# First stage in sweeps over half tiles, with 128-byte table pieces, and the last half stored in two pieces

## The chip, the cores and the metric

The kernel runs on one core of a Trainium2 chip. The metric is the device time of one execution in microseconds. The engines are TensorE (PE in the profile, with PEld for its weight loads), VectorE (DVE), ScalarE (ACT), GpSimd (POOL) and SyncE (SP); SP and ACT also issue DMA transfers, each on a queue of its own that is worked off in order.

## What is computed

One layer of a decoder: `h = x + RMSNorm_post(mixer(RMSNorm_pre(x)))` with 512 tokens of 1024 numbers, all in fp32. The mixer is a sparse attention with 16 heads in 4 groups and three branches: over compressed keys and values, over selected blocks, and over a window. With 512 tokens every block is selected. The parts that matter here:

```
u = rms_norm(x, pre_gain)
q, kv, g, z = split(u @ w_in)
kc = compress_kv(k_c, k_pos, k_w1, k_w2)     # blocks of 32 tokens, stride 16:
vc = compress_kv(v_c, v_pos, v_w1, v_w2)     # silu((block + pos) @ w1) @ w2
bias = table[t5_bucket(dist)]                # one table 32 x 16, for all three branches
o = three softmax branches; y = sum(sigmoid(g) * o * silu(z)); out = x + rms_norm(y @ w_out, post_gain)
```

## The kernel before

Every product is made of three matmuls, since fp32 operands are split in a high part (rounded to fp32r) and a low part (what is left): high by high, low by high, high by low. The normed input is kept as `uh` and `ul`, transposed, features on partitions. Weights come in tiles of 128 x 4 x 256 (512 KB) through `load_raw` into three buffers `wr`; `split_raw` casts the high part `wh` and subtracts to the low part `wl`, each with three buffers. A list `order` names the first twenty tiles: two for compressed keys (w0, w1), two for compressed values (w2, w3), then in turn four tiles for the attention values and four of the key MLP, and so on. In `split_ahead` even tiles have their high part cast on ScalarE and their low part on GpSimd, odd ones both on VectorE.

The first stage does this. `rms(t)` squares a tile of 128 tokens on ScalarE (L306) and takes the reciprocal root on GpSimd (L86, L90). `prep(t)` scales it on VectorE by that and by the gain, which lies in two PSUM banks (L316), transposes it on TensorE (L321), and splits it on ScalarE (L327) and VectorE (L328). The projection of compressed keys runs in two halves of 256 tokens, over all eight feature tiles (L247 to L249), so the first half needs input tiles 0 and 1 and both weight tiles, and tiles 2 and 3 are prepared inside it. `tables()` is called behind the first half: it multiplies the bias table with one-hot rows into `toep` (L344, L345) and, in sixteen matmuls of 16 columns (L351, L352), into `cb`; both are stored to DRAM (`toepd`, L347; `cmpb`, L356, in pieces of 16 bytes) and read back in the form of `bias` and `cbs` tiles by `load_bias(0)` (L163, L168). After the second half of keys come the position rows (`load_pos`), the key blocks (`blocks`, L407: eight VectorE operations that read the two banks of keys, then splits on ScalarE, VectorE and GpSimd), the projection of compressed values with 512 columns at a time (`half_t`), and the value blocks. Then follows the projection of attention values (L480 to L482, four banks) in turn with the key MLP (L425 to L427). The rest, attention woven with further projections, and the output projection, follows an order that a planner in the code writes out.

The end: `wout` closes the four token tiles in the order 0, 3, 2, 1. For the last one, two VectorE operations (L874, 512 columns each) add the residual, and each is followed by a store of 256 KB on SP's queue.

Engines work their queues in order. The framework orders instructions by its own estimate of time, except those pinned by `keep_in_program_order`.

Of the kernel before, what the change touches and what calls it, by code (L numbers as in the profile page):

```python
# [19 lines left out]
S = 512  # L20
# [3 lines left out]
G = 4  # L24
# [27 lines left out]
def nsa_layer(ctx: ExitStack, tc: tile.TileContext, x, pre_gain, post_gain, table, w_in, w_out,  # L52
# [39 lines left out]
    uh = [keep.tile([128, 2, S], F32R, name=f"uh{i}", tag="u", bufs=8) for i in range(4)]  # L92
    ul = [keep.tile([128, 2, S], F32R, name=f"ul{i}", tag="u", bufs=8) for i in range(4)]
# [46 lines left out]
    def proj_t(w, m, p):  # L140
        hi, lo = w
        ms = slice(m * 128, m * 128 + 128)
        for k in range(KT):
            a, b = hi[k // 4][:, k % 4, ms], lo[k // 4][:, k % 4, ms]
            rh, rl = uh[k // 2][:, k % 2, :], ul[k // 2][:, k % 2, :]
# [105 lines left out]
    def half_t(n, kh, banks):  # L251
        h, l = tile_(n)
        for kk in range(4):
            k = kh * 4 + kk
            for m, p in enumerate(banks):
                ms = slice(m * 128, m * 128 + 128)
                pass3(p, h[:, kk, ms], l[:, kk, ms], uh[k // 2][:, k % 2, :], ul[k // 2][:, k % 2, :],
                      k == 0, k == KT - 1)

    with tc.tile_pool(name="a1", bufs=1) as a1:  # L260
# [38 lines left out]
        banks = [tb, ob, tb]  # L299
        nb_ = 0  # L300

        rs_ = {}

        def rms(t):
            ss = a1.tile([128, 1], F32, name="ss", bufs=4)
            tc.keep_in_program_order(A.activation(sq, xs[t], AF.Square, scale=1.0 / 32, accum_out=ss))  # L306
            r = a1.tile([128, 1], F32, name="r", bufs=4)
            rstd(r, ss)
            rs_[t] = r

        def prep(t):
            nonlocal nb_
            r = rs_[t]
            for kq in range(2):
                hs = slice(kq * 512, (kq + 1) * 512)
                V.scalar_tensor_tensor(xs[t][:, hs], xs[t][:, hs], r, gain[kq], op0=ALU.mult, op1=ALU.mult)  # L316
                p = banks[nb_ % 3]()
                nb_ += 1
                for j in range(4):
                    k = kq * 4 + j  # L320
                    T.transpose(p[:, j * 128:(j + 1) * 128], xs[t][:, k * 128:(k + 1) * 128], ident)  # L321
                for jj in range(2):
                    i = kq * 2 + jj
                    src = p[:, jj * 256:(jj + 1) * 256].rearrange("p (a b) -> p a b", a=2)
# [702 lines left out]
```

## Time and profile before

| | us |
|---|---|
| median of three runs (lowest, highest) | 466.47 (466.29, 467.47) |
| the profiled execution | 466.85 |
| its span (first to last instruction of the profile) | 465.0 |
| TensorE busy in the span | 450.9 |
| VectorE, ScalarE, GpSimd busy | 330.6, 274.3, 184.7 |

All times in the profile count from the start of the span. A row of a timeline gives start, duration and, in brackets, how long the engine had been idle and what it waited for. Matmuls overlap, so the pace is read from start to start and not from the duration. The granted clock (PEclk) is 1.00 at TensorE's upper level, 2.4 GHz, and 0.50 at the lower one, 1.2 GHz.

### The profile page before, as it was taken

How to read it: one execution, taken by the hardware profiler on the slowest of the kernel's cores; microseconds unless marked ns; L12 is line 12 of the kernel's file. 1: busy time of each engine (PE TensorE's matmuls, PEld its weight loads, DVE VectorE, ACT ScalarE, POOL GpSimd, SP SyncE). 2: the span in 40 equal slices, each digit the busy share in tenths (PEclk: the TensorE clock that was granted, in tenths of full speed). 3: DMA queues.
4: the chain of work that ended last, by engine and by line, in shares of the span. 5: the costliest groups of instructions: out<-in, count | busy, mean ns of one | idle time of the engine just before them, and what ended most of it. 6: DMA issues, size and time to landing. Idle time of an engine off the chain costs nothing.

```text
span 465.0 us, 6924 instructions
## 1 busy us (share of the span) xinstructions
PE 450.9 (97%) x2330; PEld 375.3 (81%) x2330; DVE 330.6 (71%) x801; ACT 274.3 (59%) x642; POOL 184.7 (40%) x185
## 2 busy tenths in 40 slices
PE   5999999999999999999999999999999999999994
PEld 4797888878888878888888788888878888888883
DVE  6869844851766888768769776885896667567685
ACT  5712232542766577767846867666776666467541
POOL 4424544242223453342463525245343342448212
PEclk9989999999999999999999999999999999999998
DMA  8489275263111321511132332024051211214113
GB/s 300 142 82 280 77 216 162 66 206 90 47 45 48 112 59 34 182 45 47 45 90 70 88 94 71 21 57 132 19 180 45 92 45 47 91 43 140 47 45 135
DMA packets 45501, 44.63 MB, mean 96 GB/s; under 512 B 7751, under 2 KB 38471, under 8 KB 45466
## 3 DMA queue, kind: packets, MB, share of 16 engines
q1 hardware_dynamic: 44424, 44.00, 31.9%
q8 instruction: 18, 0.29, 0.3%
q10 hardware_dynamic: 1042, 0.20, 0.2%
q14 instruction: 17, 0.14, 0.1%
HBM read 41.99 MB, written 2.20 MB: 95 GB/s over the span
## 4 chain that ended last, share of the span: by engine, by line
PE 89%; DVE 4%; ACT 3%; issue 2%; POOL 1%; DVEq 0%; POOLq 0%; ACTq 0%
PE ps_pj L146 11%; PE ps_pj L148 11%; PE ps_pj L147 11%; PE ps_s L591 9%; PE ps_t L681 7%; PE ps_o L715 4%; PE ps_o L714 4%; PE ps_pj L834 3%; PE ps_pj L835 3%; PE ps_pj L836 3%; PE ps_s L247 2%; PE ps_s L248 2%; PE ps_s L249 2%; PE ps_pj L247 2%; PE ps_pj L248 1%
## 5 line engine op out<-in xcount | busy, mean ns | idle before, releaser
L118 POOL TENSOR_TENSOR wl<-wr,wh 128x512 fp32r<-128x512 f32 x94 | 123.0, 1328 | 138.6 <-ACT wh L113 122.2
L146 PE MATMUL ps_pj<-uh,wh 128*128 128x512 f32 x240 | 99.0, 412 | 0.0
L148 PE MATMUL ps_pj<-ul,wh 128*128 128x512 f32 x240 | 94.2, 393 | 0.0
L147 PE MATMUL ps_pj<-uh,wl 128*128 128x512 f32 x240 | 94.2, 392 | 0.0
L604 ACT ACTIVATE p<-p,nm 128x512 f32<-128x512 f32 (+3 forms) x128 | 71.6, 560 | 24.3 <-DVE nm L603 23.5
L685 DVE TENSOR_TENSOR ptl<-ps_t,pth 128x512 fp32r<-128x512 f32 x80 | 55.0, 688 | 28.2 <-ACT pth L684 27.7
L113 ACT CAST wh<-wr 128x1024 fp32r<-128x1024 f32 x47 | 49.2, 1047 | 43.5 <-DMA wr<-in_nsa_w_in_dram 20.1
L591 PE MATMUL ps_s<-kd,q 128*128 128x512 f32 (+5 forms) x256 | 63.9, 336 | 0.7 <-DVE zs L699 0.6
L684 ACT CAST pth<-ps_t 128x512 fp32r<-128x512 f32 x80 | 46.4, 580 | 29.3 <-PE ps_t L681 28.7
L148 PEld LDWEIGHTS ps_pj<-ul,wh 128*128 128x128 f32 x240 | 45.1, 188 | 10.1
L591 PEld LDWEIGHTS ps_s<-kd,q 128*128 128x128 f32 x256 | 43.9, 189 | 9.0 <-DVE zs L699 1.2
L146 PEld LDWEIGHTS ps_pj<-uh,wh 128*128 128x128 f32 x240 | 45.2, 188 | 6.1
L147 PEld LDWEIGHTS ps_pj<-uh,wl 128*128 128x128 f32 x240 | 45.3, 189 | 5.8
L603 DVE CUSTOM_DVE_ANT_0 p<-ps_s,bias 128x128 f32<-128x128 f32 (+3 forms) x80 | 34.6, 447 | 20.7 <-PE ps_s L591 20.5
L681 PE MATMUL ps_t<-ident,p 128*128 128x128 f32 x320 | 48.4, 272 | 0.0
L681 PEld LDWEIGHTS ps_t<-ident,p 128*128 128x128 f32 x320 | 39.7, 140 | 9.4
L714 PE MATMUL ps_o<-pth,vt 128*128 128x512 f32 x80 | 33.7, 421 | 0.0
L603 DVE CUSTOM_DVE_ANT_1 p<-ps_s,bias 128x256 f32<-128x256 f32 (+2 forms) x48 | 26.3, 555 | 9.3 <-PE ps_s L591 8.6
L728 POOL TENSOR_TENSOR y<-otmp,zs 128x256 f32<-128x256 f32 x16 | 12.3, 771 | 51.5 <-DVE otmp L725 51.5
L715 PE MATMUL ps_o<-ptl,vt 128*128 128x512 f32 x80 | 32.3, 404 | 0.0
L730 POOL TENSOR_TENSOR otmp<-otmp,zs 128x256 f32<-128x256 f32 x15 | 11.1, 741 | 37.9 <-DVE otmp L725 37.9
L569 ACT ACTIVATE zs<-ps_pj 128x512 f32<-128x512 f32 x22 | 13.1, 596 | 19.4 <-PE ps_pj L148 19.3
(268 smaller groups left out, 895.6 us busy)
## 6 DMA issues: line engine op xcount, KB each, us to landing
wr<-in_nsa_w_in_dram SPq DMA_DIRECT2D x36, 512.0 KB
wr<-in_nsa_w_in_dram SPq DMA_DIRECT2D x16, 256.0 KB
bias<-toepd SPq DMA_DIRECT2D x16, 256.0 KB
wr<-in_nsa_w_out_dram SPq DMA_DIRECT2D x8, 512.0 KB
xt<-in_x_dram SPq DMA_DIRECT2D x4, 512.0 KB
wr<-in_nsa_cmp_k_w_dram SPq DMA_DIRECT2D x4, 512.0 KB
wr<-in_nsa_cmp_v_w_dram SPq DMA_DIRECT2D x4, 512.0 KB
xr<-in_x_dram SPq DMA_DIRECT2D x8, 256.0 KB
```

What stands on the lines that cost most here:

```text
L113: A.copy(h[:, 0:kn], raw[:, 0:kn])
L118: el.tensor_tensor(l[:, ks], raw[:, ks], h[:, ks].bitcast(F32), op=ALU.subtract)
L146: T.matmul(p, a, rh, start=k == 0, stop=False)
L147: T.matmul(p, b, rh, start=False, stop=False)
L148: T.matmul(p, a, rl, start=False, stop=k == KT - 1)
L591: T.matmul(po, qs[h][:, qt * 128:(qt + 1) * 128], kds[h // R][:, i, c0:c0 + n], start=i == 0, stop=i == 1)
L603: V.tensor_tensor_reduce(pd, src, bi, 1.0, BIG, ALU.add, ALU.min, st["nm"][:, hh:hh + 1])
L604: A.activation(po, po, AF.Exp, bias=st["nm"][:, hh:hh + 1], scale=-1.0, accum_out=st["rs"][:, hh:hh + 1])
L681: T.transpose(tp[:, hh * 128:(hh + 1) * 128], st["p"][hh][:, c:c + 128], ident)
L685: V.tensor_tensor(pl, tp, ph.bitcast(F32), op=ALU.subtract)
L714: T.matmul(acc, v, ph, start=j == 0, stop=False)
L715: T.matmul(acc, v, pl, start=False, stop=j == qt)
```

## The change

The input tiles 0 and 1 come in halves of 512 features, w1 comes behind tile 2, and w2 behind tile 3. Of tile 0's square the second half is made on VectorE. `uh` and `ul` are two tiles of four feature tiles each instead of four of two, and one cast and one subtraction split 512 columns at a time. The projection runs in sweeps, each of one weight tile, one half of the features and 256 tokens: 24 matmuls, first high by high, then `ul` by high, then `uh` by `wl`. The sweeps go keys 0, keys 1, values 0 on the first 256 tokens, then the same on the last 256. Everything in the stage is pinned in program order. The value banks are now of the kind `o`; since half of each is written first, a matmul of a zero row opens each (`open_`). `tables()` comes behind the sixth sweep, its matmuls before and inside the second half of the value projection; the stores come behind that, `cmpb` in pieces of 128 bytes, and `load_bias(0)` is called behind the attention values. Odd tiles from the fifth on have their high part cast on ScalarE, tile 3 is split on ScalarE and GpSimd. At the end the last half is made in two operations of 256 columns, the first stored by ScalarE's queue, the second by SP's.

```
-            tiles.append(split_raw(raws[i], 4, *((V, V) if i % 2 else (A, P))))
+            tiles.append(split_raw(raws[i], 4, *((A, V) if i % 2 and i > 3 else (A, P))))
...
+        zrow = a1.tile([1, 128], F32R, name="zrow")
+        V.memset(zrow.bitcast(F32), 0.0)
         for t in range(NT):
             xt = a1.tile([128, D], F32, name="xt", bufs=4)
-            SP.dma_start(xt, x[t * 128:(t + 1) * 128, :])
+            for c in ((slice(0, 512), slice(512, D)) if t < 2 else (slice(0, D),)):
+                SP.dma_start(xt[:, c], x[t * 128:(t + 1) * 128, c])
             xs.append(xt)
-            if t == 1:
-                load_ahead(1)
+            if t:
+                load_ahead(t - 1)
...
+            for c, acc in ((0, ss), (512, s2)):
+                xc, junk = xs[t][:, c:c + 512], sq[:, c:c + 512]
+                if t == 0 and c:
+                    put(V.tensor_tensor_reduce(junk, xc, xc, 1.0 / D, 0.0, ALU.mult, ALU.add, acc))
+                else:
+                    put(A.activation(junk, xc, AF.Square, scale=1.0 / 32, accum_out=acc))
+            rstd(rs_[t], ss, s2)
...
+        def open_(ps_):
+            for p in ps_:
+                put(T.matmul(p, zrow, gh[:, 0:S], start=True, stop=False))
+
+        def sweep(n, ps_, kq, hs, opened=False):
+            h, l = tiles[n]
+            for w, u in ((h, uh), (h, ul), (l, uh)):
+                for kk in range(4):
+                    for m, p in enumerate(ps_):
+                        put(T.matmul(p[:, hs], w[:, kk, m * 128:(m + 1) * 128], u[kq][:, kk, hs],
+                                     start=not opened and kq == 0 and w is h and u is uh and kk == 0,
+                                     stop=kq == 1 and w is l and kk == 3))
+                yield
...
+        norm(1, 1, ob)
+        low(1, 0)
+        p_kc = [pj(), pj()]
+        run(sweep(0, p_kc, 0, h0))
...
+        run(sweep(0, p_kc, 0, h1))
+        with tc.issue_after(behind[0]):
+            kpt = load_pos("k")
+            vpt = load_pos("v")
+        run(sweep(1, p_kc, 1, h1))
+        kb = blocks(p_kc, kpt)
+        run(sweep(2, p_vc, 0, h1, True))
+        with tc.issue_after(behind[0]):
+            tables()
...
-        p_vc = [sb(), sb()]
-        half_t(2, 0, p_vc)
         half_t(3, 1, p_vc)
-        vb = blocks(p_vc, vpt)
-        kw2h, kw2l = load_w2("k", 2)
-        vw2h, vw2l = load_w2("v", 1)
+        SP.dma_start(toepd, toep)
+        for g in range(G):
+            SP.dma_start(dview(cmpb, g * H * MC * R, [[8 * R, 128], [1, 8 * R]]),
+                         small["cb"][:, g].rearrange("p j r -> p (j r)"))
+        vb = block_split(blocks(p_vc, vpt))
...
+        load_bias(0)
         hs = silu2(p_mk)
...
-        for i in range(2):
-            finish(*prev, i)
+        t, xr, ss = prev
+        finish(t, xr, ss, 0)
+        for c, q_ in ((0, A), (256, SP)):
+            cs = slice(c, c + 256)
+            last(V.scalar_tensor_tensor(xr[1][:, cs], g3[1][:, cs], ss, xr[1][:, cs], op0=ALU.mult, op1=ALU.add))
+            q_.dma_start(out[t * 128:(t + 1) * 128, S + c:S + c + 256], xr[1][:, cs])
```

What this does to the order of instructions is shown at three places. The first is TensorE at the start, from its first transposes on; `xt` is an input tile, `ps_t` and `ps_o` are banks for transposes, `ps_pj` the banks of compressed keys. Before:

```order
L321 MATMUL ps_t<-ident,xt 128x128 x4
L321 MATMUL ps_o<-ident,xt 128x128 x4
L321 MATMUL ps_t<-ident,xt 128x128 x4
L247 MATMUL ps_pj<-uh_80,wh 128x256
L248 MATMUL ps_pj<-uh_80,wl 128x256
```

and now:

```order
L349 MATMUL ps_t<-ident,xt 128x128 x8
L349 MATMUL ps_o<-ident,xt 128x128 x8
L386 MATMUL ps_pj<-uh_80,wh 128x256 x8
L386 MATMUL ps_pj<-ul_82,wh 128x256 x8
L386 MATMUL ps_pj<-uh_80,wl 128x256 x8
L386 MATMUL ps_pj<-uh_81,wh 128x256 x8
L386 MATMUL ps_pj<-ul_83,wh 128x256 x8
L349 MATMUL ps_t<-ident,xt 128x128 x4
L386 MATMUL ps_pj<-uh_81,wl 128x256 x8
L349 MATMUL ps_t<-ident,xt 128x128 x4
L379 MATMUL ps_o<-gh,zrow 128x512 x2
L386 MATMUL ps_o<-uh_80,wh 128x256 x8
```

The matmuls stand in runs of eight of one kind, the fourth group of transposes has moved ahead of the first matmul, and those of tile 2 stand between runs.

The second place is VectorE between the key blocks (`blk<-ps_pj`) and the value blocks (`blk<-ps_s`, now `ps_o`); `toep` and `cb` are the tables, `bl` the low parts of blocks. Before:

```order
L407 TENSOR_TENSOR blk<-ps_pj,ptk 64x16x31 x8
L115 CAST wh<-wr 128x1024
L118 TENSOR_TENSOR wl<-wr,wh 128x512
L417 TENSOR_TENSOR bl<-blk,bh 128x496 x2
L118 TENSOR_TENSOR wl<-wr,wh 128x512
L407 TENSOR_TENSOR blk<-ps_s,ptv 64x16x31 x8
```

and now:

```order
L274 TENSOR_TENSOR blk<-ps_pj,ptk 64x16x31 x8
L407 COPY toep<-ps_s 16x512
L407 COPY toep<-ps_s 16x128
L118 TENSOR_TENSOR wl<-wr,wh 128x512 x2
L414 COPY cb<-ps_s 128x8x4x4
L499 TENSOR_TENSOR bl<-blk,bh 128x496 x2
L274 TENSOR_TENSOR blk<-ps_o,ptv 64x16x31 x8
```

The three table copies, which stood ahead of the key blocks, have moved behind them, and the cast has gone.

The third place is SP's queue around the table transfers; `wr` are weight tiles, of which those of 128x2x256 come in pairs and are the tiles of attention values. Before:

```order
L103 DMA wr<-in_nsa_w_in_dram 128x2x256 x2
L103 DMA wr<-in_nsa_cmp_k_w_dram 128x4x256
L347 DMA toepd<-toep 16x640
L356 DMA cmpb<-cb 128x8x4 x4
L163 DMA bias<-toepd 128x512 x4
L168 DMA cbs<-cmpb 128x1x128 x4
L103 DMA wr<-in_nsa_w_in_dram 128x2x256 x2
```

and now:

```order
L537 DMA toepd<-toep 16x640
L103 DMA wr<-in_nsa_w_in_dram 128x2x256
L539 DMA cmpb<-cb 128x32 x4
L103 DMA wr<-in_nsa_w_in_dram 128x2x256
L163 DMA bias<-toepd 128x512 x2
L103 DMA wr<-in_nsa_cmp_k_w_dram 128x4x256
L163 DMA bias<-toepd 128x512 x2
L168 DMA cbs<-cmpb 128x1x128 x4
L163 DMA bias<-toepd 128x512 x2
L103 DMA wr<-in_nsa_w_in_dram 128x2x256 x2
L103 DMA wr<-in_nsa_cmp_k_w_dram 128x4x256
```

Before, the stores and the first loads of tables stood behind the first pair; now they stand around the third pair and the third MLP tile, ahead of the fourth pair.

## Rows read from the trace of the kernel before

**Rows 1.** Page, part 1: busy us (share of the span) xinstructions.
```profile
PE 450.9 (97%) x2330; PEld 375.3 (81%) x2330; DVE 330.6 (71%) x801; ACT 274.3 (59%) x642; POOL 184.7 (40%) x185
```

**Rows 2.** Stretches: us, PE, PEld, DVE, ACT, POOL busy; PEclk, DMA share, GB/s.
```profile
0.00:10.00 10.00, 5.15 (x16) 3.55 (x16) 6.05 (x16) 5.66 (x10) 4.07 (x14) 1.00 0.85 306
```

**Rows 3.** Timeline of PE: start, us, engine, line, names, shapes, count [idle before <-releaser].
```profile
6.96 1.12 PE L321 MATMUL ps_t<-ident,xt 128*128 128x128 f32 x4 [1.92 <-DVE xt L316]
...
7.86 1.06 PE L321 MATMUL ps_o<-ident,xt 128*128 128x128 f32 x4
...
10.24 0.58 PE L247 MATMUL ps_pj<-uh,wh 128*128 128x256 f32 x1 [0.46 <-ACT uh L327]
...
16.51 0.66 PE L321 MATMUL ps_o<-ident,xt 128*128 128x128 f32 x4 [0.41 <-DVE xt L316]
...
16.92 0.36 PE L248 MATMUL ps_pj<-uh,wl 128*128 128x256 f32 x1
...
19.16 0.63 PE L321 MATMUL ps_t<-ident,xt 128*128 128x128 f32 x4 [0.57 <-issue]
...
22.77 0.27 PE L351 MATMUL ps_s<-nth,hcr 33*128 33x16 f32 x1
...
24.64 0.58 PE L247 MATMUL ps_pj<-uh,wh 128*128 128x256 f32 x1
...
28.01 0.32 PE L247 MATMUL ps_pj<-uh,wh 128*128 128x256 f32 x1
...
41.94 0.39 PE L480 MATMUL ps_pj<-wh,uh 128*128 128x512 f32 x1
...
44.98 0.47 PE L480 MATMUL ps_s<-wh,uh 128*128 128x512 f32 x1 [0.61 <-DVE blk L407]
...
63.41 0.40 PE L480 MATMUL ps_pj<-wh,uh 128*128 128x512 f32 x1
```

**Rows 4.** Timeline of PE, more rows for the pace of matmuls.
```profile
28.17 0.28 PE L248 MATMUL ps_pj<-uh,wl 128*128 128x256 f32 x1
...
30.44 0.28 PE L249 MATMUL ps_pj<-ul,wh 128*128 128x256 f32 x1
...
32.39 0.39 PE L247 MATMUL ps_s<-uh,wh 128*128 128x512 f32 x1
```

**Rows 5.** Stretch behind the narrow table matmuls.
```profile
25.00:26.00 1.00, 1.00 (x6) 1.00 (x6) 0.72 (x4) 0.00 (x0) 0.35 (x1) 0.50 0.26 71
```

**Rows 6.** Timelines of ACT, DVE, DVE and POOL at the start.
```profile
4.00 1.06 ACT L306 ACTIVATE sq<-xt 128x1024 f32<-128x1024 f32 x1 [1.23 <-DMA xt<-in_x_dram]
...
2.92 1.27 DVE L293 TENSOR_TENSOR gl<-grow,gh 1x512 fp32r<-1x512 f32 x2
...
6.15 2.18 DVE L316 SCALAR_TENSOR_TENSOR xt<-xt,r,ps_s 128x512 f32<-128x512 f32 x3 [1.96 <-POOL r L90]
...
5.24 0.22 POOL L86 TENSOR_SCALAR r<-ss 128x1 f32<-128x1 f32 x1 [3.92 <-ACT sq L306]
```

**Rows 7.** Groups by form, 0:45: xcount | busy us, mean ns | idle
```profile
L407 DVE TENSOR_TENSOR blk<-ps_pj,ptk 64x496 f32<-64x496 f32 x8 | 5.4, 672 | 0.1
```

**Rows 8.** Timeline of PE, last wait for a weight tile.
```profile
91.89 0.38 PE L427 MATMUL ps_o<-wl,bh 128*124 128x256 f32 x1 [0.36 <-DVE wl L118]
```

**Rows 9.** Timeline of SP: issue of table loads and of the fourth value tile.
```profile
28.34 2.50 SPq L163 DMA_DIRECT2D bias<-toepd  x4
...
30.88 5.54 SPq L168 DMA_DIRECT2D cbs<-cmpb  x4
...
55.70 0.88 SPq L103 DMA_DIRECT2D wr<-in_nsa_w_in_dram  x2
```

**Rows 10.** Stretches at the end of the span.
```profile
462.25:462.50 0.25, 0.00 (x0) 0.00 (x0) 0.00 (x0) 0.00 (x0) 0.00 (x0) 0.50 0.64 246
...
463.00:463.25 0.25, 0.00 (x0) 0.00 (x0) 0.00 (x0) 0.00 (x0) 0.00 (x0) 0.50 1.04 385
...
463.75:464.00 0.25, 0.00 (x0) 0.00 (x0) 0.00 (x0) 0.00 (x0) 0.00 (x0) 0.50 0.04 8
```

More of the change, by code (lines that the diff above doesn't have):

```diff
@@ L298, in nsa_layer @@
         sq = a1.tile([128, D], F32, name="sq")
-        banks = [tb, ob, tb]
-        nb_ = 0
-        rs_ = {}
+        put = tc.keep_in_program_order
+        rs_, pt_, behind = {}, {}, []
         def rms(t):
             ss = a1.tile([128, 1], F32, name="ss", bufs=4)
[L306 to L324, printed above, removed]
-                    dh = uh[i][:, :, t * 128:(t + 1) * 128]
-                    dl = ul[i][:, :, t * 128:(t + 1) * 128]
-                    A.copy(dh, src)
-                    V.tensor_tensor(dl, src, dh.bitcast(F32), op=ALU.subtract)
@@ new lines, in rms, with scale, turn_, norm @@
+            rstd(rs_[t], ss, s2)
+        def scale(t, kq):
+            xt = xs[t][:, kq * 512:(kq + 1) * 512]
+            put(V.scalar_tensor_tensor(xt, xt, rs_[t], gain[kq], op0=ALU.mult, op1=ALU.mult))
+        def turn_(t, kq, home):
+            xt = xs[t][:, kq * 512:(kq + 1) * 512]
+            p = pt_[t, kq] = home()
+            for j in range(4):
+                put(T.transpose(p[:, j * 128:(j + 1) * 128], xt[:, j * 128:(j + 1) * 128], ident))
+        def norm(t, kq, home):
+            scale(t, kq)
+            turn_(t, kq, home)
@@ new lines, in part, with high, low, split_first @@
+        def part(u, t, kq):
+            return u[kq][:, :, t * 128:(t + 1) * 128], pt_[t, kq].rearrange("p (a b) -> p a b", a=4)
+        def high(t, kq):
+            put(A.copy(*part(uh, t, kq)))
+        def low(t, kq):
+            d, p = part(ul, t, kq)
+            i = put(V.tensor_tensor(d, p, part(uh, t, kq)[0].bitcast(F32), op=ALU.subtract))
+            behind[:] = [i.ins]
+        def split_first(n, el=P):
+            h = wp.tile([128, 4, 256], F32R, name="wh", tag="wh", bufs=3)
+            l = wp.tile([128, 4, 256], F32R, name="wl", tag="wl", bufs=3)
+            put(A.copy(h, raws[n]))
+            tiles.append((h, l))
+            def rest(i):
+                ks = slice(i * 2, i * 2 + 2)
+                put(el.tensor_tensor(l[:, ks], raws[n][:, ks], h[:, ks].bitcast(F32), op=ALU.subtract))
+            return rest
@@ L365, in nsa_layer @@
+        high(0, 0)
+        norm(0, 1, tb)
+        w0 = split_first(0)
+        w0(0)
+        w0(1)
+        norm(1, 0, ob)
+        low(0, 0)
+        high(1, 0)
+        norm(1, 1, ob)
+        low(1, 0)
+        p_kc = [pj(), pj()]
+        run(sweep(0, p_kc, 0, h0))
+        high(0, 1)
+        high(1, 1)
+        low(0, 1)
+        low(1, 1)
         rms(2)
+        w1 = split_first(1, V)
+        w1(0)
+        w1(1)
         rms(3)
[L367 to L379 removed]
+        w2 = split_first(2)
@@ new lines, in nsa_layer @@
+        w2(0)
+        w2(1)
+        s1 = sweep(1, p_kc, 1, h0)
+        next(s1)
+        next(s1)
+        norm(2, 0, tb)
+        high(2, 0)
+        run(s1)
+        norm(2, 1, tb)
+        high(2, 1)
+        scale(3, 0)
+        low(2, 0)
+        low(2, 1)
+        p_vc = [ob(), ob()]
+        open_(p_vc)
+        s2 = sweep(2, p_vc, 0, h0, True)
+        next(s2)
+        turn_(3, 0, tb)
+        high(3, 0)
+        scale(3, 1)
+        next(s2)
+        turn_(3, 1, tb)
+        high(3, 1)
@@ L798, in split_y @@
             else:
-                yhl[g] = [keep.tile([128, 2, S], F32R, name=f"y3{i}", tag="u", bufs=8) for i in range(2)]
+                t = keep.tile([128, 2, 2, S], F32R, name="y3", tag="u", bufs=4)
+                yhl[g] = [t[:, i] for i in range(2)]
         sl = slice(qt * 128, (qt + 1) * 128)
@@ L821, in wout @@
         turn = [0, 3, 2, 1]
-        og = [keep.tile([128, D], F32, name="og", tag="u", bufs=8) for _ in range(NT)]
+        og = [t[:, i] for t in [keep.tile([128, 2, D], F32, name="og", tag="u", bufs=4) for _ in range(2)] for i in range(2)]
         sumsq = const.tile([128, NT, 2], F32, name="sumsq")
```

102 lines of the change are left out of this document (49 added, 53 removed).

## The prediction

> **What bounds the kernel now.** I read the page's busy times first: TensorE is busy for 450.9 of 465.0 us [rows 1], so all idle time together is 14 us, and a change to order and transfers can win back only a part of that. Then the stretches: 4.85 us of it lie in the first 10 us [rows 2]. Then TensorE's timeline: the first projection matmul starts at 10.24 and the first matmul of the value projection (L480) at 41.94 [rows 3]; I call these 31.70 us the first stage. Inside it the reader is to see three kinds of loss. Idle ones: 0.41 us before 16.51 and 0.57 before 19.16, where transposes of tiles 2 and 3 wait [rows 3]. Slow ones: 16 table matmuls of 16 columns run from 22.77 to 24.64, and behind them 15 matmuls of 256 columns take the 3.37 us to 28.01 [rows 3], 0.22 us each, while the granted clock is 0.50, the 1.2 GHz level [rows 5]; from 28.17 to 30.44 nineteen steps of the same kind take 0.1195 us each [rows 4]. So the lower clock cost 3.37 - 15 x 0.1195 = 1.58 us. And small ones where transposes, tables and matmuls alternate. After the stage there are two idle places left that matter: 0.61 us before 44.98, for a PSUM bank that VectorE's block copies hold, and 0.36 before 91.89, for a low half of a weight tile [rows 3, 8].
>
> From the value projection on, the order of TensorE's instructions is the same in both kernels but for the places of a few matmuls in its first group. So I forecast the first stage, carry its gain through as a shift, and look for what could break the shift.
>
> **The start.** Halving the input lets the squares start on half a tile, but the last half still lands at 4.00 us, when ScalarE starts now [rows 6], because the same bytes come in the same order. VectorE takes the second half of tile 0 and is busy with the gain's low half until 4.19 [rows 6]; one 512-column pass is 0.73 us (2.18 for three [rows 6]), so it ends at 4.95, where before the squares released GpSimd at 5.24 [rows 6]. The rstd on GpSimd took 0.91 us from 5.24 to VectorE's start at 6.15 [rows 6]. The first transposes then start at about 6.7 instead of 6.96 [rows 3], 0.25 us earlier. That gain is lost again: the sweep begins only behind all sixteen transposes of tiles 0 and 1, where before the first matmul followed twelve. VectorE's new order is three scales, a low half, the fourth scale: 5.9 + 3 x 0.73 = 8.1, a wait for ScalarE's 512-column cast until 8.5, then 0.69 for the low half (a 512-element pass of this kind is bounded by 0.67 [rows 7] and 0.73) and 0.73 for the scale give 9.9; four transposes take 0.9 us (6.96 to 7.86 [rows 3]). The first sweep starts at about 10.8, 0.6 us later than now.
>
> **The first stage itself.** From there TensorE has to do: 144 matmuls of 256 columns (96 for keys, 48 for the first half of values) x 0.1195 = 17.2; 24 of 512 columns for the second half of values x 0.2274 (32.39 to 41.94 in 42 steps [rows 3, 4]) = 5.5; four groups of four transposes at 0.41 (16.51 to 16.92 [rows 3]) = 1.6; the two zero matmuls that open the value banks, 2 x 0.2274 = 0.45; the sixteen narrow ones 1.87 (22.77 to 24.64); the four wide table matmuls and two small transposes by the same pace 0.9; two matmuls at the lower clock before it rises, 0.2. Sum 27.7. Of this the zero matmuls are new, and so is the cutting of the first half of values: 48 x 0.1195 against 24 x 0.2274 is 0.28 us more. The Trainium skill's TensorE: Matmul & The Clock Gate (section "Wait — 56ns, not 53.3ns?") puts the fixed cost of one more warm matmul at about 2.5 ns; by it the cutting would cost an estimated 0.06 us and the sum would be 0.2 lower. The rows here give 11 ns per cut, and I stay with them.
>
> Waits: the scale of tile 2 stands behind the low half of the second weight tile on VectorE, which I work out to hold TensorE for 0.15 us. At the end a new one appears. The narrow table matmuls need a bank that VectorE's copy of the first table empties, and that copy now stands behind the eight block copies of the keys (0.672 each, 5.4 us [rows 7]). These start when the fifth sweep ends, at about 28.1, so the table copy ends at 34.25; TensorE comes there, after the sixth sweep (2.9), the wide tables (0.7) and ten matmuls (2.3), at 33.9, and waits 0.4. With 0.4 us for changes between kinds of matmul (what the old stage lost beside the waits named, about) the stage takes 27.7 + 0.15 + 0.4 + 0.4 = 28.65 us and ends at 10.8 + 28.65 = 39.45 against 41.94: **2.5 us** saved. Of these, 1.58 is the low clock, 0.98 the two idle places, the rest of the old alternation pays for the later start and the new matmuls.
>
> **What hides the rest.** The casts of odd weight tiles move from VectorE to ScalarE; VectorE loses about 0.7 us each, ScalarE has room (274 us busy of 465 [rows 1]). The cover for VectorE's work is the second half of values: it must finish key blocks, table copies, one low half and two low block parts before the value blocks can start; I get about 39.3 against TensorE's 39.45, so the 0.61 us bank wait stays as it is, and each 0.1 us that VectorE is later adds 0.1. The bound is 0.7 on one side (one more pass of that kind [rows 7]) and nothing on the other, since the bank wait can't start before TensorE is there. The 0.36 us before 91.89 should go: VectorE's chain of kd parts and that low half has one cast of 0.7 us less in it. Bounds 0 to 0.36; I take 0.36.
>
> **The end.** The last half is written in two pieces on two queues. The last two stores move 512 KB without a gap from 462.25 to 463.75 at 246 to 385 GB/s, and 1.2 us pass between the last bytes and the span's end [rows 10]. The bytes, their start (the first store is unchanged) and the last VectorE result stay, so the end of the transfer stays: 0. If smaller last pieces did shorten the path, the bound is half a store's time, 128 KB at about 370 GB/s = 0.35 us gain; if the second queue costs something, about as much loss.
>
> **Sum.** 2.5 + 0.36 + 0 = 2.85 us off the profiled execution's 466.85 (span 465.0 and 1.85 around it) is 464.0. The median of the three runs is 466.47, 0.38 lower, inside their spread of 1.2 us, so I don't shift for it fully and say **464.1**.
>
> **Rivals.** *The clock falls again* behind the narrow table matmuls. For it: they stand together again, with the 0.4 us wait ahead of them, so the quiet stretch is 2.3 us instead of 1.87. Against: at their old place tables, transposes and matmuls also alternated, and now full matmuls stand right before and behind. Price 1.58 less the little that VectorE's lag gives back: 464.1 + 1.5 = 465.6. *The low clock lasts through the first sweep* because TensorE's first 10 us stay thin: 24 matmuls at 0.22 instead of 0.1195 cost at most 2.3, with half of that 465.3, with all 466.4. *The sweeps don't close the gaps*: ScalarE or VectorE is the bound between 11 and 21 us (a sweep's weight cast stands behind a square of 1.06 us [rows 6] on ScalarE) and each of the six sweeps waits 0.4: 464.1 + 2.4 = 466.5, no change. *Weights wait behind tables* (the slower side). SyncE's queue is in order, and the fourth value tile's load now stands behind six bias and four cbs loads, with the four cmpb stores a little ahead. Before, four and four of these kept the queue for 2.50 + 5.54 us [rows 9], and the fourth value tile's load, issued at 55.70, was used at 63.41, 7.7 us later [rows 9, 3]. In the new kernel that use would be at 39.45 + 21.5 = 60.9, so the load must go by 53.2. The table loads follow the third MLP tile, at about 43.7; at the old pace (8.0 + 0.9 for two more bias loads) they are through at 52.6, 0.6 in time. The mechanism decides from there, 1 us for 1 us; at 1.6 times the old pace it costs 4.8: 468.9. Against it: the 16-byte pieces of cmpb that filled the DMA engines before are now 128 bytes and an eighth as many, and the wait for their completion was part of the 5.54. The Trainium skill's DMA: Bandwidth & Descriptors (section "Specifications") holds against this that transfers under 512 B are below line rate, which 128 B still is; by that rule the stores would stay dear, and the loads behind them late, which is this rival; no row here shows 128-byte pieces.
>
> **How the numbers follow.** Forecast (clock stays up) 0.47; clock falls again 0.30; long low clock at the start 0.08; gaps stay 0.07; weights behind tables 0.08. About 0.3%, 1.4 us, is what a measurement of this kernel can tell from no change: 465.07 and 467.87 are the edges. Faster: nearly all of the first, a quarter of the second, half of the third, 0.57. Slower: the last, with a little for the unforeseen, 0.09. Between: 0.34. The range runs from the forecast less the tail's 0.35 and an error of 0.6 in a stage of 28.65 us, 463.2, up through the second and most of the third case, 466.2; it leaves out the rest of the third, the fourth and the last.
>
> **What would show it.** First sweep's start near 10.8 and unbroken 256-column matmuls at 0.12 us; first value-projection matmul near 39.5 (41 if the clock fell, with 0.50 in the stretches after the narrow matmuls); a wait of 0.4 us on VectorE before the first narrow one; the bank wait still about 0.6; no wait before the last key-value MLP tile; the same distance of 1.2 us from the last byte to the end. Wrong it would be if the order that is the same behind the first stage met new waits on weights, or if the first sweeps waited for casts.

## The result, and the profile after

The changed kernel takes 470.09 us (median of six runs, 469.85 to 472.86), the kernel before 467.37 in the same session: a ratio of 1.0079, with a 95% interval from 1.0055 to 1.0102. It is some 3 us slower (2.7 by the medians, 3.7 by the ratio), where I had forecast 2.4 us faster, and outside my range. The profiled execution took 470.27 us (span 468.5), 3.4 more than that of the kernel before, and TensorE is busy for 3.5 us more than in [rows 1]:

```profile
PE 454.4 (97%) x2356; PEld 378.9 (81%) x2356; DVE 321.4 (69%) x784; ACT 283.7 (61%) x647; POOL 186.2 (40%) x187
```

So the time is not lost in waits alone: TensorE itself works longer. Where, its timeline shows. The rows answer to those of the first stage in [rows 3]; the columns are start, duration, engine, line, names, shapes and count.

```profile
7.19 1.97 PE L349 MATMUL ps_t<-ident,xt 128*128 128x128 f32 x8 [2.15 <-DVE xt L343]
9.92 2.37 PE L349 MATMUL ps_o<-ident,xt 128*128 128x128 f32 x8 [0.76 <-DVE xt L343]
11.94 1.78 PE L386 MATMUL ps_pj<-uh,wh 128*128 128x256 f32 x8
13.56 1.11 PE L386 MATMUL ps_pj<-ul,wh 128*128 128x256 f32 x8
...
36.29 0.40 PE L412 MATMUL ps_s<-nth,hcr 33*128 33x16 f32 x1
...
40.19 0.49 PE L248 MATMUL ps_o<-uh,wl 128*128 128x512 f32 x1
...
40.91 0.63 PE L247 MATMUL ps_o<-uh,wh 128*128 128x512 f32 x1
41.33 0.63 PE L248 MATMUL ps_o<-uh,wl 128*128 128x512 f32 x1
...
45.08 0.39 PE L563 MATMUL ps_pj<-wh,uh 128*128 128x512 f32 x1
```

The first sweep starts at 11.94, 1.7 us later than the first projection matmul before; its first eight matmuls take 1.62 us, 0.20 each, before the pace of 0.12 is reached; the granted clock there (12 to 14 us, first row below) reads 1.00, so the profile names no low clock for it. From then on the sweeps run as forecast, unbroken, to 33 us. The sixteen narrow table matmuls take 3.90 us (36.29 to 40.19), where they took 1.87 before. Behind them 512-column matmuls follow each other at 0.42 us (40.91 to 41.33) instead of 0.23, and the granted clock of these stretches falls from 1.00 to 0.51, the 1.2 GHz level (the clock is the third number from the end):

```profile
12.00:14.00 2.00, 2.00 (x14) 2.00 (x13) 1.64 (x3) 1.82 (x5) 0.53 (x1) 1.00 0.91 224
...
38.00:40.00 2.00, 2.00 (x10) 2.00 (x10) 0.00 (x0) 0.00 (x0) 0.00 (x0) 1.00 0.47 124
40.00:42.00 2.00, 2.00 (x7) 1.66 (x7) 0.97 (x3) 1.66 (x4) 0.99 (x2) 0.64 0.19 36
42.00:44.00 2.00, 2.00 (x6) 1.54 (x6) 1.31 (x1) 0.47 (x1) 2.00 (x2) 0.51 0.76 126
```

Fourteen 512-column matmuls stand between 40.19 and 45.08: 4.89 us instead of 14 x 0.2274 = 3.18, so the fall cost 1.7. The value projection starts at 45.08, 3.14 us later than before. The wait for a value bank shrinks (VectorE has more time), and by 94 us the kernel is only 2.5 us behind (94.35 against 91.89 [rows 8]). But at 167 us it is 3.2 behind again. These are the first of the gate matmuls (`wgs`) and the row at 167 us, in the kernel before and in the changed one:

```profile
99.38 0.40 PE L522 MATMUL ps_s<-uh,wgs 128*96 128x512 f32 x1
...
163.91 0.44 PE L698 MATMUL ps_s<-ident,f 128*128 128x128 f32 x2 [0.27 <-DVE nm L603]
```

```profile
101.82 0.40 PE L606 MATMUL ps_s<-uh,wgs 128*96 128x512 f32 x1
...
167.12 0.44 PE L782 MATMUL ps_s<-ident,f 128*128 128x128 f32 x2 [0.26 <-DVE nm L687]
```

Two waits of TensorE lie around the gate matmuls; the second is new. The rows are from the timelines of TensorE, ScalarE, GpSimd, SyncE and VectorE, in order of time:

```profile
91.28 1.05 ACT L113 CAST wh<-wr 128x1024 fp32r<-128x1024 f32 x1
...
92.46 2.98 POOL L118 TENSOR_TENSOR wl<-wr,wh 128x512 fp32r<-128x512 f32 x2 [8.38 <-ACT wh L113]
...
94.35 0.39 PE L509 MATMUL ps_o<-wl,bh 128*124 128x256 f32 x1 [0.31 <-DVE wl L118]
95.46 9.27 SPq L103 DMA_DIRECT2D wr<-in_nsa_w_in_dram  x5
99.42 1.05 ACT L113 CAST wh<-wr 128x1024 fp32r<-128x1024 f32 x1 [5.19 <-DMA wr<-in_nsa_w_in_dram]
...
105.77 0.42 DVE L515 SCALAR_TENSOR_TENSOR hs<-th,ps_o 124x256 f32<-124x256 f32 x1
...
106.25 0.43 PE L521 MATMUL ps_t<-ident,hs 124*128 124x124 f32 x2 [0.55 <-DVE hs L515]
```

Read as a chain: ScalarE casts a weight tile at 91.28, GpSimd makes its low half until 95.44, that frees the buffer, SyncE issues the next load at 95.46, it lands, ScalarE casts it at 99.42, and VectorE comes to `hs` late, for which TensorE waits 0.55 us. The start and the end of the span come with the experiments on them.

### The profile page after: what moved, and what is told of

It reads as the page before. It is cut to its first block, busy times and chain, and to the rows that moved or that the text cites. A ratio compares the mean times of both kernels' runs of the same rounds, so it can differ in the third digit from the quotient of the medians.

```text
span 468.5 us, 6984 instructions
## 1 busy us (share of the span) xinstructions
PE 454.4 (97%) x2356; PEld 378.9 (81%) x2356; DVE 321.4 (69%) x784; ACT 283.7 (61%) x647; POOL 186.2 (40%) x187
## 4 chain that ended last, share of the span: by engine, by line
PE 85%; DVE 7%; ACT 3%; DMA 2%; issue 1%; POOL 0%; SPq 0%; POOLq 0%; DVEq 0%; ACTq 0%
PE ps_pj L146 11%; PE ps_pj L148 11%; PE ps_pj L147 11%; PE ps_s L675 8%; PE ps_t L765 7%; PE ps_o L799 4%; PE ps_o L798 4%; PE ps_pj L919 3%; PE ps_pj L920 3%; PE ps_pj L921 3%; PE ps_pj L386 3%; PE ps_s L782 1%; PE ps_s L247 1%; PE ps_s L248 1%; PE ps_s L249 1%
## 5 line engine op out<-in xcount | busy, mean ns | idle before, releaser
L118 POOL TENSOR_TENSOR wl<-wr,wh 128x512 fp32r<-128x512 f32 x92 | 120.2, 1326 | 138.1 <-ACT wh L113 109.1
L113 ACT CAST wh<-wr 128x1024 fp32r<-128x1024 f32 x55 | 57.5, 1047 | 44.6 <-PE ps_s L249 13.5
L118 DVE TENSOR_TENSOR wl<-wr,wh 128x512 fp32r<-128x512 f32 x18 | 16.6, 957 | 13.6 <-ACT wh L113 13.4
```

Of the source, the lines that this page charges most:

```text
L113: A.copy(h[:, 0:kn], raw[:, 0:kn])
L118: el.tensor_tensor(l[:, ks], raw[:, ks], h[:, ks].bitcast(F32), op=ALU.subtract)
```

## The experiments

Four of the first five each undo one part of the changed kernel; they ran beside the same runs of the kernel before (median 466.99). The other, second below, adds one part of the change to the kernel before.

**Neighbouring columns for the narrow matmuls.** My theory was that the 128-byte pieces made them dear: to lay eight rows side by side, each matmul takes every eighth column of the one-hot rows as its stationary operand.

```
-            put(A.copy(hcr, hotc))
+            put(A.copy(hcr, hotc.rearrange("p (m j) -> p j m", j=8)))
...
-                T.matmul(p[:, j * H:(j + 1) * H], hcj[:, j], nth, start=True, stop=False)
+                T.matmul(p[:, j * H:(j + 1) * H], hcr[:, j], nth, start=True, stop=False)
```

> The changed kernel, but the one-hot rows are put in the order of the narrow table matmuls while they are cast, so that each of the sixteen reads a stationary of 128 neighbouring columns instead of every eighth; the 128-byte pieces stay. Theory (the strided read of the stationary makes them dear): the sixteen go from 3.90 us back to about 1.9, and the kernel from 470.1 to about 468.1. Rival (they are slow where they stand, for instance since two accumulating matmuls follow each other on one bank): 3.9 us again, 470.1. On the clock: if the fall behind them is due to their length, it goes too and the kernel comes to 466.5; if a stretch of 1.9 us is enough, as before the change, the matmuls behind them stay at 0.43 us.

Measured: 468.42 us, ratio 1.0019 (0.9991 to 1.0048), in two groups of five, 465.9 to 467.3 and 469.6 to 470.0. The weight loads of eight of the sixteen (the other eight take the same), grouped by form in the changed kernel and then in this one (count, busy us, mean ns of one):

```profile
L413 PEld LDWEIGHTS ps_s<-ntl,hcr 33*128 33x128 f32 x8 | 2.7, 332 | 0.0
```

```profile
L412 PEld LDWEIGHTS ps_s<-ntl,hcr 33*128 33x128 f32 x8 | 1.5, 188 | 0.0
```

A load of 128 columns takes 188 ns from neighbouring columns and 331 ns from every eighth; the stretch is 1.9 us again. The theory holds. The cast that now does the reordering takes 2.15 us instead of 1.05 on ScalarE, where nobody waits for it. The Trainium skill's SBUF — State Buffer (the note on 16-byte cachelines in the section "Door 1: The DMA port swizzle") says that a read which enters a new line with each access pays, so that fp32 can be strided without cost over 4 elements; a stride of 8 is beyond that. The trace agrees, in both operations; no run has a stride between 1 and 8, so where the limit lies is not shown. On the clock the run decides nothing: the profiled execution, of the upper group, has the fall (512-column matmuls at 0.43 from 40.89 on) and its whole first sweep slow (24 matmuls in 4.8 us); the lower group has no profile.

**The strided stationary alone, in the kernel before** (run later, beside a median of 467.21): the 128-byte pieces and nothing else.

```
-                T.matmul(p[:, j * H:(j + 1) * H], hcr[:, j * 128:(j + 1) * 128], nth, start=True, stop=False)
+                T.matmul(p[:, j * H:(j + 1) * H], hcj[:, j], nth, start=True, stop=False)
...
-                SP.dma_start(dview(cmpb, g * H * MC * R, [[R, 128], [128 * R, 8], [1, R]]), cb[:, g])
+                SP.dma_start(dview(cmpb, g * H * MC * R, [[8 * R, 128], [1, 8 * R]]), cb[:, g].rearrange("p j r -> p (j r)"))
```

> The kernel before with one part of the change alone: the 128-byte pieces of cmpb, with the strided stationary that they bring. Theory (the strided read costs wherever the narrow matmuls stand): the sixteen take 3.9 us instead of 1.87 and the time is 468.5 against 466.6. Rival (the slow narrow matmuls have to do with their new place): 1.9 us and 466.6. The issue of the stores and of the loads of cbs, 3.17 and 5.54 us, shrinks to about 1.8 and 2.6 in either case.

Measured: 470.32 us, ratio 1.0065 (1.0042 to 1.0088). The sixteen run from 23.98 to 27.8, so at their old place too:

```profile
23.98 0.40 PE L352 MATMUL ps_s<-nth,hcr 33*128 33x16 f32 x1
...
27.57 0.38 PE L353 MATMUL ps_s<-ntl,hcr 33*128 33x16 f32 x1
```

With the pieces alone the old kernel is nearly as slow as the changed one, by 3 us. The narrow matmuls show 2 of these. In this profile 1.2 more are lost ahead of them, where the edit touches nothing: the first projection matmul starts at 10.74 (0.5 late), and the narrow ones at 23.98 instead of 22.77. What costs that is open.

**Odd weight tiles cast on VectorE again.**

```
-            tiles.append(split_raw(raws[i], 4, *((A, V) if i % 2 and i > 3 else (A, P))))
+            tiles.append(split_raw(raws[i], 4, *((V, V) if i % 2 and i > 3 else (A, P))))
```

> The changed kernel, but odd weight tiles from the fifth on have their high part cast on VectorE again. Theory (ScalarE's queue, in which these casts now stand behind the casts of kd, starts the next even tile late, its buffer comes free late and its load lands late): the cast that waits for a load at 99.42 moves to about 97, the wait of 0.55 us before the transposes of hs at 106.25 goes, the distance to the kernel before at 167 us shrinks from 3.2 to about 2.5, and the time goes from 470.1 to 469.4; the wait of 0.3 at 94.35 stays as it is before the change. Rival (the load is late because SyncE's queue had the tables): all of that stays, 470.1.

Measured: 470.51 us, ratio 1.0074 (1.0047 to 1.0101): no gain in the time, and still the theory is right where it speaks. Its timelines:

```profile
48.49 0.47 PE L563 MATMUL ps_o<-wh,uh 128*128 128x512 f32 x1 [0.30 <-DVE blk L274]
...
95.45 0.38 PE L509 MATMUL ps_o<-wl,bh 128*124 128x256 f32 x1 [0.36 <-DVE wl L118]
...
98.33 1.05 ACT L113 CAST wh<-wr 128x1024 fp32r<-128x1024 f32 x1 [5.55 <-DMA wr<-in_nsa_w_in_dram]
...
102.92 0.40 PE L606 MATMUL ps_s<-uh,wgs 128*96 128x512 f32 x1
...
106.63 0.38 PE L521 MATMUL ps_t<-ident,hs 124*128 124x124 f32 x2
...
167.44 0.44 PE L782 MATMUL ps_s<-ident,f 128*128 128x128 f32 x2 [0.26 <-DVE nm L687]
```

This execution started its first sweep 0.5 us later and reached the gate matmuls at 102.92 instead of 101.82; from there to the row at 167 us it needs 64.52 us, the changed kernel 65.30, the kernel before 64.53. The cast that waits for a load is at 98.33, 4.6 us ahead of the gate matmuls instead of 2.4, and the wait before `hs` is gone: 0.78 us. The other profiles say the same: the wait before `hs` is 0.4 to 0.8 us in the six with these casts on ScalarE, and missing in the nine with them on VectorE. But the wait for a value bank is back: the matmul at 48.49 starts 0.68 us after the one before it, against 0.36 in the changed kernel and a pace of 0.23. What VectorE takes over late, it lacks early. The wait of 0.36 before the low half stays.

**Whole input tiles.**

```
-            for c in ((slice(0, 512), slice(512, D)) if t < 2 else (slice(0, D),)):
+            for c in (slice(0, D),):
```

> The changed kernel, but tiles 0 and 1 of the input come whole, one transfer each; squares, scales and all orders stay. Theory (four half transfers land later than two whole ones: the second half of tile 1 at 7.3 us, where the whole tile was there at 5.4 before): tile 0 is there at about 4.0 and tile 1 at 5.4, the first sweep starts at about 10.6 instead of 11.94, and the time goes from 470.1 to 468.8. Rival (it is VectorE's and GpSimd's order of scales and roots that sets the start): the first sweep stays at 11.5 to 12, 470.

Measured: 469.36 us, ratio 1.0049 (1.0031 to 1.0067), 1.4 us better by the ratios and 0.7 by the medians. ScalarE's squares show when the input landed, first of the changed kernel, then of this one:

```profile
3.35 0.63 ACT L338 ACTIVATE sq<-xt 128x512 f32<-128x512 f32 x1 [0.58 <-DMA xt<-in_x_dram]
...
7.31 0.63 ACT L338 ACTIVATE sq<-xt 128x512 f32<-128x512 f32 x1 [1.36 <-DMA xt<-in_x_dram]
```

```profile
4.13 0.63 ACT L338 ACTIVATE sq<-xt 128x512 f32<-128x512 f32 x1 [1.36 <-DMA xt<-in_x_dram]
...
5.51 0.63 ACT L338 ACTIVATE sq<-xt 128x512 f32<-128x512 f32 x1 [0.66 <-DMA xt<-in_x_dram]
```

With halves the first is there at 3.35, but the last, of tile 1, at 7.31; whole, tile 1 is there by 5.51. The first sweep starts at 11.03. Four halves also take SyncE 1.80 us to issue, two whole tiles 0.85, so everything behind them starts 0.95 later. Since starts differ from execution to execution, a clean pair follows below.

**The last half in one piece.**

```
-        t, xr, ss = prev
-        finish(t, xr, ss, 0)
-        for c, q_ in ((0, A), (256, SP)):
...
+        for i in range(2):
+            finish(*prev, i)
```

> The changed kernel, but the last half is made in one operation of 512 columns and stored on one queue, as before the change. Theory (the two pieces cost): from the last matmul to the end of the span 6.6 us instead of 6.9, from the last byte to the end 1.2 instead of 1.5, 469.8. Rival (the end is the same either way): 470.1. Rival (pieces help, and the end is slower without them): 470.4.

Measured: 470.74 us, ratio 1.0085 (1.0057 to 1.0113), nothing that the time can tell. The profiles can: from the start of TensorE's last matmul to the span's end it is 6.75 to 6.9 us in six profiles of kernels with two pieces (6.9 in five of them) and 6.5 to 6.75 in nine with one; the changed kernel and this one, which differ in the pieces alone, have 6.88 and 6.70. So the pieces gain nothing and cost some 0.2 to 0.3. In the changed kernel the last bytes move until 467.0 of 468.5:

```profile
466.50:467.00 0.50, 0.00 (x0) 0.00 (x0) 0.00 (x0) 0.00 (x0) 0.00 (x0) 1.00 0.90 307
467.00:467.50 0.50, 0.00 (x0) 0.00 (x0) 0.00 (x0) 0.00 (x0) 0.00 (x0) 0.73 0.01 2
```

They pass at 300 to 380 GB/s, near the rates of [rows 10], and 1.5 us follow the last byte instead of 1.2. That agrees with the Trainium skill's DMA: Bandwidth & Descriptors (section "Issuing engines are not separate DMA queues"): transfers issued by two engines share the same DMA engines, and only issue time is saved.

**Narrow matmuls between wide ones.** To keep the clock up I put the sixteen, with neighbouring columns, one by one between the last fourteen 512-column matmuls.

```
+                    put(T.matmul(p, w[:, kk, ms], u[1][:, kk, :], start=False, stop=kk == 3 and u is ul))
+                    i += 1
+                    if i > 10:
+                        next(tab, None)
```

> The kernel of e1_contig (neighbouring columns for the narrow matmuls), but the sixteen narrow matmuls stand one by one between the last fourteen matmuls of 512 columns of the second half of values, instead of in one stretch. Theory (the clock falls behind a stretch of narrow matmuls, in most executions): no matmul of 512 columns at 0.43 us after 38 us, granted clock 1.00 through the stage, and every execution in the lower group of e1_contig, about 466.2. Rival (the clock falls because of what stands before, or by chance of the moment): falls remain in part of the executions, times from 466 to 470 again. Rival (a narrow matmul between two wide ones costs more than among its own): the last part of the stage gets longer by up to 16 x 0.1 = 1.6 us and eats the gain, 467.8.

Measured: 474.65 us, beside a median of 466.63, ratio 1.0181 (1.0156 to 1.0207), the opposite of the plan:

```profile
35.50 0.27 PE L414 MATMUL ps_s<-ntl,hcr 33*128 33x16 f32 x1
35.70 0.49 PE L488 MATMUL ps_o<-uh,wh 128*128 128x512 f32 x1
36.12 0.27 PE L412 MATMUL ps_s<-nth,hcr 33*128 33x16 f32 x1
36.33 0.50 PE L488 MATMUL ps_o<-uh,wl 128*128 128x512 f32 x1
```

At full clock one pair takes 0.62 us (35.50 to 36.12), where its two members take 0.11 and 0.23 among their own kind: 0.28 is lost in each pair. That is the last rival, almost three times as dear as I had allowed. And the clock falls inside the stretch and stays down for 13 us, though the profile shows TensorE busy throughout. Stretches of this kernel:

```profile
34.00:38.00 4.00, 4.00 (x14) 2.24 (x13) 2.17 (x5) 0.00 (x0) 0.00 (x0) 1.00 0.33 87
38.00:42.00 4.00, 4.00 (x9) 2.27 (x8) 0.00 (x0) 0.00 (x0) 0.00 (x0) 0.51 0.90 292
```

**All four undone, with the woven order, and the same with warm-up matmuls.** Two kernels stood on the wrong idea of the woven order:

> The kernel of f1_weave, and beside it the input tiles whole, the high part of odd weight tiles cast on VectorE again, and the last half stored in one piece: all four suspected losses undone, while sweeps, table place and 128-byte pieces stay. Theory (the losses add up): against the changed kernel's 470.1, minus 2.0 (narrow matmuls), 1.6 (clock), 1.35 (start), 0.78 (ScalarE's queue) and 0.2 (end), and plus 0.45 since the wait for a value bank grows back to 0.6: about 464.6, faster than the kernel before by 2 us. Rival (the losses hide each other, so that what is taken away in the stage comes back as waits for weights or banks): 466 to 467, no change.

> The kernel of f2_combo with four matmuls of 512 columns of a zero row, whose result is thrown away, in TensorE's idle time before the first transposes. Theory (the first sweep's matmuls start at the lower clock because TensorE was idle before the transposes): the first eight matmuls of the first sweep take 0.12 us each instead of 0.23, 1.0 us less, and the time is 463.6 where f2_combo has 464.6. Rival (the transposes and the gap behind them set it, not what is before them): the first eight stay at 0.23 us, no difference from f2_combo.

Measured: 473.1 us (1.0145, 1.0125 to 1.0165) and 472.53 (1.0132, 1.0107 to 1.0157). Neither says anything of the sum of the losses, since both have the woven order, with which the kernel above took 6.2 us more than with neighbouring columns alone (474.65 against 468.42). The second answers its own question: the first eight matmuls take 1.53 us behind four extra matmuls and 1.36 without. So its theory fails; that the transposes and the gap behind them set the pace, as the rival says, is not shown by that.

```
+        for i in range(4):
+            put(T.matmul(p_kc[i % 2], zrow, gh[:, 0:S], start=True, stop=True))
```

**All four undone, sixteen narrow matmuls in one stretch; and eight instead.** The next two take the narrow matmuls together again. The second stacks the table's high and low part on 97 partitions (zeros between), so that one matmul does the work of two.

```
+            nt2 = a1.tile([97, H], F32R, name="nt2")
+            V.tensor_copy(nt2[0:33], ntab)
+            V.tensor_tensor(nt2[64:97], ntab, nt2[0:33].bitcast(F32), op=ALU.subtract)
...
+                T.matmul(p[:, j * H:(j + 1) * H], hcr[:, j], nt2, start=True, stop=True)
```

> The changed kernel with its suspected losses undone as in g1_stack, but the sixteen narrow matmuls as they are, in one stretch of 1.8 us on neighbouring columns. Theory (the losses add): 470.1 - 1.9 - 1.35 - 0.78 - 0.2 + 0.4 (the bank wait that grows back) = 466.3 where the clock falls behind the narrow ones, 464.6 where it stays up; two groups of executions. Rival (they hide each other): 467.5 or more.

> The changed kernel with its suspected losses undone (neighbouring columns for the narrow matmuls, whole input tiles, odd high parts cast on VectorE, last half in one piece), and with the high and low part of the table stacked on the partitions, with zero rows between, so that one matmul over 97 rows does what two over 33 did: 8 narrow matmuls instead of 16, 2 wide ones instead of 4, in one stretch. Theory (a shorter narrow stretch leaves the clock up): stretch 0.95 us, no matmul of 512 columns at 0.43 us behind it, 463.9. Rival (the clock falls again in most executions): 465.5. Rival (the two more casts hold ScalarE and so the next weight tiles): a wait before a value-projection matmul, 466 or more.

Measured: 467.32 us (1.0001, 0.9984 to 1.0017) and 466.7 (0.9983, 0.9967 to 0.9998), beside a median of 467.21. The runs of the first fall into two groups of six, 465.9 to 466.9 and 467.7 to 468.3. The rival that the losses hide each other has its share. The eight narrow ones take 0.9 us and the clock stays up behind them, but here is VectorE's and TensorE's part of the second kernel:

```profile
36.06 0.69 DVE L115 CAST wh<-wr 128x1024 fp32r<-128x1024 f32 x1
...
41.70 5.49 DVE L274 TENSOR_TENSOR blk<-ps_o,ptv 64x496 f32<-64x496 f32 x8
...
35.88 1.06 PE L413 MATMUL ps_s<-nt,hcr 97*128 97x16 f32 x8 [0.22 <-DVE toep L409]
...
39.62 0.39 PE L563 MATMUL ps_pj<-wh,uh 128*128 128x512 f32 x1
...
44.56 0.47 PE L563 MATMUL ps_o<-wh,uh 128*128 128x512 f32 x1 [1.84 <-DVE blk L274]
```

TensorE reaches the value projection at 39.62, close to my forecast of 39.45, and then waits 1.84 us for a bank: VectorE starts the value blocks only at 41.70, and the weight cast at 36.06, which the changed kernel has on ScalarE, stands on its way there. In the first kernel that wait is 1.95, and there the clock falls behind it.

**Stacked, and nothing else undone.**

> The kernel of e1_contig with the table's high and low part stacked as in g1_stack, and nothing else undone. Theory (the length of the narrow stretch decides on the clock): all executions in the lower group of e1_contig less 1.0, about 465.2, no matmul of 512 columns at 0.43 us after 38 us. Rival (it does not): two groups again, around 465 and 469.

Measured: 466.12 us, ratio 0.9976 (0.9957 to 0.9994): eight of ten runs between 465.0 and 466.3, two at 467.5 and 468.2, so one group and a tail rather than two. Odd casts are on ScalarE here; VectorE starts the value blocks at 40.15, and the bank wait is 0.63 (the wait before `hs`, 0.77). In these two stacked kernels a memset of mine stood between the two steps of the first root on GpSimd (the first step starts at 5.17, the second at 6.56), and the first sweep starts late, at 11.90 and 11.99:

```profile
5.53 0.94 POOL L399 MEMSET hcr<- 32x1024 f32 x1
```

**Each loss at its place, and the same with halved input.** The last pair puts odd casts on ScalarE up to the twelfth tile and on VectorE from there, stacks the table, moves the memset, and closes in one piece; the two kernels differ in the input transfers alone.

```
+            tiles.append(split_raw(raws[i], 4, *((V if i > 12 else A, V) if i % 2 and i > 3 else (A, P))))
```

> The changed kernel with the table stacked (8 narrow matmuls over neighbouring columns), input tiles whole, last half in one piece, and the high part of odd weight tiles on ScalarE up to the twelfth tile (value projection, where VectorE is late for the value blocks) and on VectorE from there (where ScalarE's queue is late); the zero rows of the stacked tiles are set behind the stage's roots on GpSimd, where in g1_stack and g3_stackonly a memset of 0.94 us stood between two steps of the first root. Theory (each loss has its own place): the wait for a value bank is 0.6 as in g3_stackonly, not 1.84 as in g1_stack; the wait of 0.77 before hs goes; the first sweep starts at 11.0; 464.4, faster than the kernel before by 2.5. Rival (VectorE is the bound behind the stage and takes back what the start gains): bank wait 1.4, 465.4.

> The kernel of h1_best, but tiles 0 and 1 of the input in halves as in the changed kernel; nothing else differs. Theory (the halves land the second half of tile 1 later, at 6.3 to 8.1 in the six profiles so far against 5.4 to 6.0 for whole tiles): 0.8 us slower than h1_best, with a wider spread, first sweep at 11.0 to 12.7. Rival (the late landings came from the moment and not from the halves): the same as h1_best within 0.3.

Measured, beside a median of 467.08: 464.27 us, ratio 0.994 (0.9921 to 0.9959), 463.4 to 464.7; with halves 465.54, ratio 0.997 (0.9954 to 0.9985), 463.6 to 466.2. The first is faster than both kernels, and within 0.2 of what was expected:

```profile
11.43 1.55 PE L386 MATMUL ps_pj<-uh,wh 128*128 128x256 f32 x8
...
39.31 0.39 PE L563 MATMUL ps_pj<-wh,uh 128*128 128x512 f32 x1
...
42.58 0.47 PE L563 MATMUL ps_o<-wh,uh 128*128 128x512 f32 x1 [0.62 <-DVE blk L274]
...
89.27 0.38 PE L509 MATMUL ps_o<-wl,bh 128*124 128x256 f32 x1 [0.35 <-DVE wl L118]
```

The bank wait is 0.62, the wait before `hs` is gone, the clock stays at 1.00 from 20 to 56 us. Halving the input costs 1.3 us by the medians, and the spread grows from 1.3 (six runs) to 2.6 us (twelve). The profiled execution with halves was its fastest (463.56), with tile 1's second half there at 6.48; so the halves do not always cost, but over the runs they do.

## Why the prediction was wrong, point by point

**First sweep at 10.8**: 11.94, 1.1 late. The step that failed is "the last half still lands at 4.00 us [...] because the same bytes come in the same order". Tile 0's second half was there at 4.52, tile 1's at 7.31. I had counted bytes and not transfers. With whole tiles the sweep starts at 10.9 to 11.4 in the profiles without the memset, so the rest of that paragraph's working holds within 0.6. In two of the seven profiles with halves it starts as early (10.89 and 10.94).

**"The sixteen narrow ones 1.87"**: 3.90, and this is the largest single error, 2.0 us. I saw the 128-byte pieces as a matter of DMA and did not ask how the rows come to lie side by side. The strided slice stands in `tables()`, but in the part of the diff that my cut left out, and the order shows the same operation and shape before and after.

**Clock**: the rival with 0.30 came true, at 1.7 us against a price of 1.58. Of the profiled executions with the sixteen narrow matmuls in one stretch, all but one had the fall right behind them (in that one, with all four undone, it came later, behind the bank wait); of the four with eight stacked ones none had it. Those kernels differ in other things too (the nearest pair is the first experiment and the stacked kernel with nothing else undone), so that the stacking keeps the clock up is likely and not shown.

**The low clock in the first sweep**: a rival with 0.08; its pace came in part, its clock is not on record. The first eight matmuls cost 0.7 us more than at the full pace in the changed kernel, of which the forecast had counted 0.2; from profile to profile it is 0.1 to 0.9, and in two of them most of the first sweep was slow, 1.9 us more. There the matmuls follow at 0.21 us, as they did at the granted clock of 0.50 behind the narrow ones [rows 3, 5], but the granted clock of the first sweep reads 1.00 in every profile. So whether it is the clock is not shown. What decides is open; four matmuls ahead of the transposes did not change it.

**The stage**: 28.65 us forecast, 33.14 measured from the first sweep on. The error of 4.5 is the narrow matmuls (2.0), the clock (1.7) and the first sweep (0.5 beyond the 0.2 counted); 0.3 is left, which no row names. The other sweeps, transposes and zero matmuls were sized rightly, the wait of 0.4 for the table copy was about 0.2.

**The bank wait of 0.61 "stays as it is"**: the step into that bank took 1.00 us before (43.98 to 44.98) and 0.36 in the changed kernel (47.12 to 47.48), since TensorE was late. That gave 0.6 back. The bound was right in kind and too small: the wait grew to 1.84 and 1.95, by 1.2 and 1.3 instead of 0.7, as soon as TensorE was early and VectorE had one cast more.

**"ScalarE has room"**: failed. The queue is in order, and the odd tile's cast put the next even tile's cast behind the kd casts; 0.78 us, by the experiment. A share of busy time says nothing of what stands behind what.

**The 0.36 before the low half "should go"**: it did not, in any of the profiles, whichever engine casts odd tiles. So the cast does not set it; what does was not tried.

**The end, 0 within 0.35**: 0.2 to 0.3 lost, inside the bound.

**Weights behind tables** (the slower side, 0.08): did not happen; TensorE waits for no weight tile in the value projection. The stores of `cmpb` before, then these stores and the loads of `cbs` in the changed kernel:

```profile
25.07 3.17 SPq L356 DMA_DIRECT2D cmpb<-cb  x4
```

```profile
40.62 1.84 SPq L539 DMA_DIRECT2D cmpb<-cb  x4
...
50.55 2.56 SPq L168 DMA_DIRECT2D cbs<-cmpb  x4
```

Stores and loads take SyncE 1.84 and 2.56 us instead of 3.17 and 5.54 [rows 9]; with the pieces alone, in the kernel before, 1.82 and 2.55. So the stores did not stay as dear as the rival had it by the rule on transfers under 512 B in the Trainium skill's DMA: Bandwidth & Descriptors (section "Specifications"): pieces of 128 bytes were cheaper here than those of 16. These are issue times on SyncE, not rates of the transfers.

In sum: 1.1 (start) + 4.5 (stage) - 0.6 (bank) + 0.3 (low half) + 0.8 (ScalarE's queue) + 0.3 (end) = 6.4 on top of 464.0 is 470.4; the profiled execution took 470.27. Three of the steps that failed have their cause shown by experiments: the landing of the halves, the price of the narrow matmuls and the room on ScalarE. The fall of the clock was foreseen as a rival, and what brings it on stays open.

## What to carry to other kernels

Where a layout for a transfer changes, follow it back to the operand that must then be read with a stride, and cost that read, too. A queue in order has room only if nothing that is waited for stands behind the new work, so ask of each moved instruction what comes next on that engine. And a gain at TensorE is worth only what the engine that frees its banks can follow: look where that engine's chain ends before and after.

## What the runs showed of the hardware that I had not expected

A 16-column matmul over 33 rows between two of 512 columns over 128 rows cost 0.28 us more per pair than the two among their own kind, and in all three kernels with such an alternation the granted clock fell to 0.50 inside it while the profile shows TensorE 100% busy. A weight load of 128 fp32 columns took 331 ns with a stride of eight columns and 188 ns without. Matmuls of 256 columns can follow at 0.21 us, the pace of the lower level, while the granted clock reads 1.00, as in the first sweep of the first experiment. Two transfers of 256 KB are not one of 512 KB: with the input of two tiles in halves, the last half was there at 6.3 to 8.1 us in seven profiles, the second tile as a whole by 5.4 to 6.0.
